# Moving every tile that a rounded float32 matmul reads to a multiple of 512 bytes

## The chip, the cores and the metric

The kernel runs on one core of one Trainium2 chip. The metric is the device time of one launch in microseconds (us). A difference of about 0.2%, some 3.5 us here, is the least that a measurement of this kernel can tell from no change.

## What is computed

The reference is a trunk of two layers on 1,024 tokens of width 1,024, in float32. Each layer is `h = h + W_out(mixer(rmsnorm(h)) * silu(gate))`, and a last norm follows. Layer 0 is a state-space mixer, layer 1 a retention mixer:

```
h = x
for i in range(DEPTH):                      # DEPTH = 2
    hn = _rmsnorm(h, norm_g)
    y = _ssd_mixer(hn, *p) if i == 0 else _retention_mixer(hn, positions, *p)
    h = h + y
return _rmsnorm(h, final_norm)
...
z, xbc, dt = _split(h @ w_in, (SSD_DI, SSD_CONV_DIM, SSD_HEADS))   # layer 0: 1024 -> 6176
q, k, v, g = _split(h @ w_in, (1024, 1024, 2048, 2048))            # layer 1: 1024 -> 6144
return y.astype(h.dtype) @ w_out                                   # both: 2048 -> 1024
```

Layer 0 puts `xbc` through a convolution of four taps and runs 8 groups of heads over 8 chunks of 128 tokens. Layer 1 rotates `q` and `k` and runs 4 heads over the same chunks, carrying a 256 x 512 state per head.

## The kernel before

**Three matmuls for one product.** To come near float32 with matmuls that read a rounded float32 (the type `float32r`), both operands are split: ACT writes the rounded value `hi`, DVE the rest `lo = src - hi` (`split`, L102 to L104). `mm3` (L137 to L140) then adds `hi*hi` (L138), `hi*lo` (L139) and `lo*hi` (L140) in one PSUM bank. Each of these matmuls streams 512 columns of the moving operand (2,048 bytes of each partition) past a stationary operand of 128 x 128 (512 bytes of each partition), and each loads its stationary operand anew. The program has 6,576 of them. Its other matmuls (transposes, the mixer of layer 0, sums over partitions) read plain float32 and are 988 in the program.

**Stages.** `Layer0.run` projects with `project` (outputs `fb`, `ip`, `z`; stationary: the weights `w0h`, `w0l`; moving: the activations `hh`, `hl`) and interleaves the mixer. `OutProj.gen` multiplies by the first output matrix (`o0p`; stationary `o0h`, `o0l`; moving `o0yh`, `o0yl`). `Layer1.head` runs per head: `qk_unit` (`q`, `k`; stationary: weights `w1h`, `w1l`; moving: the activations `h1`), `block` (`g`, `v`; here the activations are stationary and the weights move), `front` and `back` (`pS`, `po`; operands `kh`, `kl`, `sh`, `sl`, `qh`, `ql` against `vh`, `vl`, `Sh`, `Sl`). The second `OutProj` ends it (`o1p`).

**Where the tiles lie.** The order of the work is settled when the program is built; pools are laid out then too. A tile takes a multiple of 32 bytes per partition. Pools without a side fill up from address 0, pools with `side="right"` fill down from 229,344. The lowest 16,384 bytes are a scratch for transfers that GpSimd would issue; the kernel has none. Behind it come 128 bytes of constants and the pool `cpool` (L918: `vec`, `con`, `ones_r`, `cst`). So the addresses of the program of before, as remainders of division by 512, are:

| pool | tiles that `mm3` reads | remainder |
|---|---|---|
| `gp` (from 19,552) | `w0h w0l o0h o0l o1h o1l`, two of five pairs of `w1h w1l` | 96 |
| `actp` (from 52,320) | `hh hl`, most of `o0yh o0yl` | 96 |
| `sbL` (from 52,320) | `vh vl kh kl sh sl qh ql Sh Sl` | 96 |
| `gB` (from 111,008) | three of five pairs of `w1h w1l` | 416 |
| `xs` (from 196,320), eight slots of 4,128 bytes | four of the `h1`, some of `o0yh o0yl o1yh o1yl` | 224, 256, ... 448 |
| `hp` (below `xs`) | the other `h1`, most of `o1yh o1yl` | 224 |
| `tmp0` (below `hp`) | one pair `o0yh o0yl` | 192 |

Within a tile every operand starts at a multiple of 512 bytes. Of the 6,576 matmuls, 3,392 have a moving and a stationary operand with the same remainder, always 96 (`fb` 48, `ip` 1,488, `z` 768, `o0p` 624, `po` 264, `pS` 168, `o1p` 32). In the other 3,184 the two remainders differ (`g` 768, `v` 768, `o1p` 736, `q` 384, `k` 384, `o0p` 144). Below, the first are called in step and the second out of step.

Of the kernel before, what the change touches and what calls it, by code (L numbers as in the profile page):

```python
# [12 lines left out]
F32 = mybir.dt.float32  # L13
# [7 lines left out]
P = 128  # L21
T = 1024
D = 1024
KT = D // P
NC = T // P
# [12 lines left out]
NV = 296  # L38
CO = dict(ident=0, tri=128, rowq=256, rowk=288, inv=320)
NCONST = 321  # L40


def two_pi_parts(bits, count):
# [53 lines left out]
def drain(gen):  # L97
    for _ in gen:
        pass
# [5 lines left out]


class WStream:
    """Weight tiles, loaded and split ahead of their use."""

    def __init__(self, nc, cx, srcs, ahead, name, pools=None):  # L110
        self.nc, self.cx, self.srcs, self.ahead, self.name = nc, cx, srcs, ahead, name
# [31 lines left out]
class Layer0:  # L143
# [28 lines left out]
        return self.sb.tile(shape, F32, tag=tag, bufs=bufs, name=name)  # L172

    def xtile(self, name):
        return self.cx.xs.tile([P, T + 3], F32, tag="xs", bufs=8, name=name)

    def load_x(self):
        nc, cx = self.nc, self.cx
# [5 lines left out]
        self.hl = [cx.act.tile([P, T], F32R, tag="act", bufs=16, name=f"hl{k}") for k in range(KT)]  # L184

    def split_x(self, h):
        """Half of the tokens: load, gain, split."""
        nc, cx = self.nc, self.cx
        sl = slice(h * HALF, (h + 1) * HALF)
        if h == 0:  # L190
            self.wdt = self.tile([P, KT * SSD_H], "xdt", 2, "wdt")
            nc.scalar.dma_start(self.wdt, cx.wdt)
        for k in range(KT):
            nc.sync.dma_start(self.xr[k][:, sl], cx.xT[k][:, sl])
            if h == 0 and k == 3:
                self.ws.prep()
            if h == 0 and k == 7:
                nc.sync.dma_start(cx.con, cx.con_src)
                self.ws.prep()
        if h == 0:  # L200
            for k in range(KT):
                gain = cx.vec[:, VO["n0"] + k : VO["n0"] + k + 1]
                ws = slice(k * SSD_H, (k + 1) * SSD_H)
                nc.vector.tensor_scalar(self.wdt[:, ws], self.wdt[:, ws], gain, None, ALU.mult)
        for k in range(KT):
            xs = self.xr[k][:, sl]
            gain = cx.vec[:, VO["n0"] + k : VO["n0"] + k + 1]
            nc.scalar.activation(self.hh[k][:, sl], xs, AF.Copy, scale=gain)
            nc.vector.scalar_tensor_tensor(
                self.hl[k][:, sl], xs, gain, self.hh[k][:, sl].bitcast(F32), ALU.mult, ALU.subtract  # L210
            )
# [27 lines left out]
        return pt  # L239

    def dt_project(self, h):
        """Sums over every fourth block of channels, in the four quarters of the partitions."""
        nc = self.nc
        sl = slice(h * HALF, (h + 1) * HALF)
        pt = self.dt_ps[h] = self.ps.tile([P, HALF], F32, tag="py", bufs=2, name=f"dt{h}")
        for k in range(KT):
            q = k % 4
            nc.tensor.matmul(
                pt[32 * q : 32 * q + 32], self.wdt[:, k * SSD_H : (k + 1) * SSD_H], self.xr[k][:, sl],
                start=k < 4, stop=k >= 4,  # L250
            )
# [234 lines left out]
    def norm(self, g, lo, hi):  # L486
# [23 lines left out]
        yield  # L510

    def run(self, tail, start):
        """All groups; `tail` is merged with the end of the last one."""
        nc, cx = self.nc, self.cx
        self.load_x()
        self.split_x(0)
        self.dt_project(0)
        self.squares(0)
        first, second = self.units([("B", 0)]), self.units([("C", 0)])
        self.first_banks = [self.ps.tile([P, HALF], F32, tag="pa", bufs=2, name=f"fb{i}") for i in range(2)]  # L520
        next(first)
        next(second)
        self.stats(0)
        self.split_x(1)
        self.dt_project(1)
        self.squares(1)
        next(first)
        next(second)
        self.stats(1)
        drain(first)  # L530
        drain(second)
        merge((self.decay(), 3), (self.units(self.steps[0][2:]), 8))
        for g in range(SSD_G - 1):
            lst = self.steps[g + 1]
            gens = [(self.ssd(g), 9), (self.units(lst), 2 * len(lst))]
            if g:
                gens.append((self.norm(g - 1, 0, T), 4))
            merge(*gens)
        g = SSD_G - 1
        s = self.ssd(g)  # L540
        start()
        merge((take(s, 5), 5), (self.units(self.steps[g + 1]), 4), (self.norm(g - 1, 0, T), 4))
        merge((take(s, 2), 2), (self.norm(g, 0, HALF), 3), (take(tail, 1), 1))
        merge((s, 2), (take(tail, 3), 3))
        merge((self.norm(g, HALF, T), 3), (tail, 4))
        self.es.close()
# [48 lines left out]


class Rope:
    """cos and sin of position times frequency, [frequency, token]."""

    def __init__(self, tc, cx, sb, tmp):  # L600
        self.nc, self.cx, self.tmp = tc.nc, cx, tmp
# [39 lines left out]
class Layer1:  # L641
# [5 lines left out]
        self.h, self.acc = {}, {}  # L647

    def take_h(self, h, d, pt):
        """The first out-projection's results: residual sum, split, squares."""  # L650
        nc, cx = self.nc, self.cx
        sl = slice(h * HALF, (h + 1) * HALF)
        res = cx.tp.tile([P, HALF], F32, tag="res", bufs=2, name=f"res{h}_{d}")
        nc.sync.dma_start(res, cx.xT[d][:, sl])
        nc.vector.tensor_tensor(res, res, pt, ALU.add)
        nc.sync.dma_start(cx.h1d[d][:, sl], res)
        gain = cx.vec[:, VO["n1"] + d : VO["n1"] + d + 1]
        pool, tag, bufs = (cx.xs, "xs", 8) if h == 0 and d < 4 else (self.hpool, "h1", 12)
        ht = pool.tile([P, 2, HALF], F32R, tag=tag, bufs=bufs, name=f"h1_{h}_{d}")
        nc.scalar.activation(ht[:, 0, :], res, AF.Copy, scale=gain)  # L660
        nc.vector.scalar_tensor_tensor(ht[:, 1, :], res, gain, ht[:, 0, :].bitcast(F32), ALU.mult, ALU.subtract)
        self.h[h, d] = ht
        sq = cx.tp.tile([P, HALF], F32, tag="sq", bufs=2, name=f"hsq{h}_{d}")
        nc.scalar.activation(sq, res, AF.Square)
        if d:
            nc.vector.tensor_tensor(sq, sq, self.acc[h], ALU.add)
        self.acc[h] = sq
# [20 lines left out]
    def start(self):  # L688
        tc, cx = self.tc, self.cx
        self.es = ExitStack()  # L690
        self.ps = self.es.enter_context(tc.tile_pool(name="psL", bufs=1, space=PSUM))
        self.sb = self.es.enter_context(tc.tile_pool(name="sbL", bufs=1, reuse_waits="tile"))
        self.gB = self.es.enter_context(tc.tile_pool(name="gB", bufs=1, reuse_waits="tile"))
        seq = []
        for h in range(RH):
            seq += [cx.w1qk[4 * h + i] for i in range(4)]
            seq += [cx.w1g[4 * h + i] for i in range(4)]
            seq += [cx.w1v[4 * h + i] for i in range(4)]
        self.ws = WStream(self.nc, cx, seq, 1, "w1", [(cx.gp, 2), (self.gB, 3)])
# [164 lines left out]


class Final:
    """The second out-projection's results: residual sum and the last norm."""

    def __init__(self, tc, cx, sb, outT):
        self.nc, self.cx, self.sb, self.outT = tc.nc, cx, sb, outT  # L870
# [40 lines left out]
def body(tc, aps):  # L911
    nc = tc.nc
# [4 lines left out]
    with ExitStack() as es:  # L917
        cpool = es.enter_context(tc.tile_pool(name="cpool", bufs=1))  # L918
# [6 lines left out]
        cx.vec = cpool.tile([P, NV], F32, name="vec")  # L925
        cx.con = cpool.tile([P, NCONST], F32, name="con")
        nc.sync.dma_start(cx.vec, aps["vec"])
# [2 lines left out]
        cx.ones = cx.ones_r.bitcast(F32)  # L930
        nc.gpsimd.memset(cx.ones, 1.0)
        cst = cpool.tile([P, 3], F32, name="cst")
        for i, (nm, v) in enumerate((("eps", EPS), ("eps4", 4 * EPS), ("halfpi", math.pi / 2))):
            nc.gpsimd.memset(cst[:, i : i + 1], v)
            setattr(cx, nm, cst[:, i : i + 1])
        cx.ysp = [cx.dram.tile([P, T], F32, name=f"ysp{k}") for k in range(16)]
        cx.osp = [cx.dram.tile([P, T], F32, name=f"osp{k}") for k in range(16)]
        cx.h1d = [cx.dram.tile([P, T], F32, name=f"h1d{k}") for k in range(KT)]
        cx.xs = es.enter_context(tc.tile_pool(name="xs", bufs=1, side="right"))

        act_es = ExitStack()
# [2 lines left out]
        l1 = Layer1(tc, cx)  # L944
# [10 lines left out]
        hpool = es.enter_context(tc.tile_pool(name="hp", bufs=1, side="right", reuse_waits="tile"))  # L955
        with tc.tile_pool(name="tmp0", bufs=1, side="right", reuse_waits="tile") as tmp:
            l1.hpool = hpool
            l1.rnat = hpool.tile([P, NC], F32, name="rnat")
            l1.rope = rope = Rope(tc, cx, hpool, tmp)
            slot = (tmp, "early", 2)  # L960
            op0.early = [(slot, slot)]
            op0.raw = lambda h: (tmp, "yraw", 3)
            merge((take(g0, 7), 7), (rope.half(0), 3))
            drain(take(g0, 5))
            merge((take(g0, 4), 4), (l1.stats(0), 2))
            merge((take(g0, 6), 6), (rope.half(1), 3))
            drain(g0)
# [8 lines left out]
        xs, h1, sg = (cx.xs, "xs", 8), (hpool, "h1", 12), (l1.sb, "Sf", 1)  # L976
# [14 lines left out]
def pack(i):  # L991
# [35 lines left out]
    out["vec"] = v  # L1027
    con = np.zeros((P, NCONST), f)
    con[:, CO["ident"] : CO["ident"] + P] = np.eye(P)
# [11 lines left out]

# [15 lines left out]
```

## Time and profile before

| | us |
|---|---|
| median of 3 runs | 1775.35 |
| lowest and highest | 1774.92 and 1775.7 |
| span of the profiled execution | 1772.9 |

The span runs from the first to the last instruction; the 2.45 us between it and the median lie around it. PE is the matmul engine and PEld its weight loads; DVE, ACT and POOL are the vector, scalar and GpSimd engines, SP issues most transfers. The duration of a matmul in the profile contains the time that it takes to come out of the array; matmuls overlap, so the step from the start of one to the start of the next is what a matmul costs, and it is shorter than the duration. In a steady run the duration is the step plus about 162 ns, so a difference of two durations is a difference of two steps.

### The profile page before, as it was taken

What the parts mean: (1) busy time and instruction counts of PE and PEld (TensorE: products, weight loads), DVE (VectorE), ACT (ScalarE), POOL (GpSimd) and SP (SyncE); (2) the same over time, 40 slices, a digit from 0 to 9 for tenths busy, and PEclk for the clock granted to TensorE, in tenths of its full rate; (3) what the DMA queues carried; (4) which work ended last, traced back from release to release, by engine and by line L of the source; (5) the groups of instructions that cost most, each with busy time, mean ns of one, the idle gap of its engine ahead of it and who ended that gap; (6) DMA issues with size and microseconds to landing.
All of it is one profiled execution on the core that took longest, in us unless ns stands there. A gap on an engine that the chain in (4) does not pass through costs nothing.

```text
span 1772.9 us, 21526 instructions
## 1 busy us (share of the span) xinstructions
PE 1728.8 (98%) x8158; PEld 1381.9 (78%) x8158; DVE 1087.5 (61%) x1889; ACT 687.8 (39%) x1106; POOL 194.4 (11%) x221
## 2 busy tenths in 40 slices
PE   8989999999999999999999999999999999999996
PEld 5777777777878787688878887888888888878785
DVE  7857876868686868878452366246615661666443
ACT  6455544454545455544331232133212322342422
POOL 3012222222222322300000000000000000000000
PEclk9999999999999999999999999999999999999998
DMA  5143322322333334565431112112111221344451
GB/s 179 52 114 85 84 96 72 95 72 96 85 82 96 77 91 115 171 213 184 149 107 36 48 42 66 36 54 65 48 33 45 66 66 48 97 141 143 143 184 71
DMA packets 91766, 166.07 MB, mean 94 GB/s; under 512 B 8592, under 2 KB 42000, under 8 KB 91664
## 3 DMA queue, kind: packets, MB, share of 16 engines
q1 hardware_dynamic: 90368, 162.49, 29.9%
q10 hardware_dynamic: 1296, 2.23, 0.3%
q8 instruction: 64, 1.05, 0.2%
q14 instruction: 38, 0.31, 0.1%
HBM read 139.38 MB, written 25.30 MB: 93 GB/s over the span
## 4 chain that ended last, share of the span: by engine, by line
PE 67%; DVE 11%; DMA 10%; ACT 8%; issue 3%; SPq 1%; DVEq 0%; ACTq 0%
DMA eab<-acd 4%; PE o1p L140 3%; PE o1p L138 3%; PE g L140 3%; PE g L138 3%; PE g L139 3%; PE o1p L139 3%; PE v L139 3%; PE v L138 3%; PE v L140 3%; DMA acb<-acd 3%; PE ip L139 3%; PE ip L140 3%; PE ip L138 3%; DVE acc L341 3%
## 5 line engine op out<-in xcount | busy, mean ns | idle before, releaser
L138 PE MATMUL ip<-hh,w0h 128*128 128x512 f32 x496 | 201.4, 406 | 0.0
L140 PE MATMUL ip<-hh,w0l 128*128 128x512 f32 x496 | 196.6, 396 | 0.0
L139 PE MATMUL ip<-hl,w0h 128*128 128x512 f32 x496 | 195.0, 393 | 0.0
L104 DVE TENSOR_TENSOR w1l<-w1r,w1h 128x1024 fp32r<-128x1024 f32 x48 | 58.3, 1222 | 149.9 <-ACT w1h L103 149.6
L341 DVE SCALAR_TENSOR_TENSOR acc<-pre,vec,acc 128x1024 f32<-128x1024 f32 x96 | 124.5, 1299 | 7.2 <-ACT acc L339 6.6
L459 POOL TENSOR_TENSOR yT<-yT,tof 128x128 f32<-128x128 f32 x112 | 108.2, 987 | 162.6 <-DVE tof L455 162.6
L422 ACT ACTIVATE acb<-acb,acum 128x128 f32<-128x128 f32 x256 | 77.0, 388 | 99.5 <-DMA acb<-acd 99.5
L905 POOL TENSOR_TENSOR h<-h,frs 128x512 f32<-128x512 f32 x2 | 2.9, 1486 | 1018.1 <-ACT frs L899 1018.1
L140 PEld LDWEIGHTS ip<-hh,w0l 128*128 128x128 f32 x496 | 93.2, 188 | 19.9 <-issue 0.7
L138 PEld LDWEIGHTS ip<-hh,w0h 128*128 128x128 f32 x496 | 93.3, 188 | 19.4 <-issue 1.1
L139 PEld LDWEIGHTS ip<-hl,w0h 128*128 128x128 f32 x496 | 93.3, 188 | 18.5 <-DVE xr L223 0.2
L138 PE MATMUL z<-hh,w0h 128*128 128x512 f32 x256 | 103.2, 403 | 1.4 <-DVE w L357 1.4
L103 ACT CAST w1h<-w1r 128x1024 fp32r<-128x1024 f32 x48 | 49.9, 1049 | 136.6 <-PE q L139 51.6
L138 PE MATMUL v<-w1h,h 128*128 128x512 f32 x256 | 102.5, 401 | 0.0
L138 PE MATMUL o0p<-o0yh,o0h 128*128 128x512 f32 x256 | 101.0, 395 | 1.3 <-ACT o0yh L103 1.0
L139 PE MATMUL o0p<-o0yl,o0h 128*128 128x512 f32 x256 | 100.5, 393 | 1.5 <-DVE o0yl L104 1.5
L140 PE MATMUL o1p<-o1yh,o1l 128*128 128x512 f32 x256 | 101.5, 397 | 0.3 <-DVE o1l L104 0.3
L140 PE MATMUL o0p<-o0yh,o0l 128*128 128x512 f32 x256 | 101.2, 395 | 0.3 <-DVE o0l L104 0.3
L139 PE MATMUL v<-w1l,h 128*128 128x512 f32 x256 | 101.5, 397 | 0.0
L138 PE MATMUL g<-w1h,h 128*128 128x512 f32 x256 | 101.2, 395 | 0.0
L138 PE MATMUL o1p<-o1yh,o1h 128*128 128x512 f32 x256 | 101.0, 395 | 0.2 <-DVE vl L764 0.2
L140 PE MATMUL v<-w1h,h 128*128 128x512 f32 x256 | 101.1, 395 | 0.0
(244 smaller groups left out, 4075.0 us busy)
## 6 DMA issues: line engine op xcount, KB each, us to landing
w0r<-w SPq DMA_DIRECT2D x48, 512.0 KB, 3.3
acb<-acd SPq DMA_DIRECT2D x16, 1024.0 KB, 8.6
o0r<-w0o SPq DMA_DIRECT2D x32, 512.0 KB, 3.5
o1r<-w1o SPq DMA_DIRECT2D x32, 512.0 KB, 3.3
eab<-acd SPq DMA_DIRECT2D x64, 128.0 KB, 9.0
o0yr<-ysp SPq DMA_DIRECT2D x32, 256.0 KB, 3.5
w1r<-w1qk SPq DMA_DIRECT2D x16, 512.0 KB, 3.3
w1r<-w1g SPq DMA_DIRECT2D x16, 512.0 KB, 3.4
```

Of the source, the lines that this page charges most:

```text
L103: nc.scalar.copy(hi, src)
L104: nc.vector.tensor_tensor(lo, src, hi.bitcast(F32), ALU.subtract)
L138: nc.tensor.matmul(ps, ahi, bhi, start=first, stop=False)
L139: nc.tensor.matmul(ps, ahi, blo, start=False, stop=False)
L140: nc.tensor.matmul(ps, alo, bhi, start=False, stop=last)
L341: nc.vector.scalar_tensor_tensor(acc, pre[:, j : j + T], cw(j), acc, ALU.mult, ALU.add)
L422: nc.scalar.activation(m[:, h, :], m[:, h, :], AF.Relu, scale=-1.0, bias=self.acum[:, col + h : col + h + 1])
L459: nc.gpsimd.tensor_tensor(yT[j][:, cs], yT[j][:, cs], tof[:, j], ALU.add)
L905: nc.gpsimd.tensor_tensor(r, r, rs, ALU.mult)
```

## The change

No instruction is added on purpose. The scratch shrinks from 16,384 to 1,024 bytes. Three padding tiles are allocated and never used: `pad` (1,952 bytes) at the end of `cpool`, `rpad` (2,016 bytes) at the top of the right side, `spad` (192 bytes) between `sbL` and `gB`. The slots of `xs` grow from 1,027 floats (4,128 bytes) to 1,152 floats (4,608 bytes, 9 x 512); `rnat` grows from 8 floats to 128 (512 bytes). By the same layout, `cpool` now ends at 6,144 (12 x 512), `xs` starts at 190,464 (372 x 512), and each pool of the table above starts at a multiple of 512: all 6,576 matmuls have the remainder 0 in both operands.

```diff
+SCRATCH = 1024
+XS = 1152
+PAD = 1952
+RPAD = 2016
...
     def xtile(self, name):
-        return self.cx.xs.tile([P, T + 3], F32, tag="xs", bufs=8, name=name)
+        return self.cx.xs.tile([P, XS], F32, tag="xs", bufs=8, name=name)
...
         self.sb = self.es.enter_context(tc.tile_pool(name="sbL", bufs=1, reuse_waits="tile"))
+        self.es.enter_context(tc.tile_pool(name="spad", bufs=1)).tile([P, 48], F32, name="spad")
         self.gB = self.es.enter_context(tc.tile_pool(name="gB", bufs=1, reuse_waits="tile"))
...
         cst = cpool.tile([P, 3], F32, name="cst")
+        cpool.tile([P, PAD // 4], F32, name="pad")
...
+        rpad = es.enter_context(tc.tile_pool(name="rpad", bufs=1, side="right"))
+        rpad.tile([P, RPAD // 4], F32, name="rpad")
         cx.xs = es.enter_context(tc.tile_pool(name="xs", bufs=1, side="right"))
...
-            l1.rnat = hpool.tile([P, NC], F32, name="rnat")
+            l1.rnat = hpool.tile([P, P], F32, name="rnat")
...
-    nc = bacc.Bacc("TRN2", target_bir_lowering=False, num_devices=1)
+    nc = bacc.Bacc("TRN2", target_bir_lowering=False, num_devices=1, dynamic_dma_scratch_size=SCRATCH)
```

## Rows read from the trace of the kernel before

**Rows 1.** The page: busy time of the engines, the granted clock, the chain.

```profile
PE 1728.8 (98%) x8158; PEld 1381.9 (78%) x8158; DVE 1087.5 (61%) x1889; ACT 687.8 (39%) x1106; POOL 194.4 (11%) x221
...
PEclk9999999999999999999999999999999999999998
...
PE 67%; DVE 11%; DMA 10%; ACT 8%; issue 3%; SPq 1%; DVEq 0%; ACTq 0%
```

**Rows 2.** PE's waits (total us, times, longest): the costliest of 17 lines.

```profile
PE pst L462 <- ACT bn L417: 13.2, 9, 3.0
```

**Rows 3.** Busy us (instructions) of each engine: layer 0, layer 1's heads.

```profile
50.00:740.00 690.00, 670.46 (x3469) 534.73 (x3468) 512.92 (x839) 338.42 (x603) 173.64 (x192) 1.00 0.33 91
...
880.00:1590.00 710.00, 707.20 (x3202) 574.24 (x3200) 351.75 (x751) 194.32 (x310) 0.00 (x0) 1.00 0.20 63
```

**Rows 4.** PE in order of time (start, duration, us): a run in step.

```profile
67.64 0.39 PE L138 MATMUL ip<-hh,w0h 128*128 128x512 f32 x1
...
73.08 0.39 PE L138 MATMUL ip<-hh,w0h 128*128 128x512 f32 x1
```

**Rows 5.** The same view: a run of `g`, out of step.

```profile
1138.95 0.39 PE L138 MATMUL g<-w1h,h 128*128 128x512 f32 x1
...
1150.13 0.39 PE L138 MATMUL g<-w1h,h 128*128 128x512 f32 x1
```

**Rows 6.** Busy us of each engine in these two runs, columns as above.

```profile
1138.95:1150.13 11.18, 11.18 (x49) 9.03 (x48) 0.00 (x0) 1.38 (x2) 0.00 (x0) 1.00 0.01 1
67.64:73.08 5.44, 5.44 (x25) 4.50 (x24) 5.08 (x7) 2.56 (x5) 0.00 (x0) 1.00 0.31 96
```

**Rows 7.** PE in order of time: a run of `k`, out of step.

```profile
1088.82 0.39 PE L138 MATMUL k<-h,w1h 128*128 128x512 f32 x1
...
1094.14 0.40 PE L140 MATMUL k<-h,w1l 128*128 128x512 f32 x1
```

**Rows 8.** Groups by line, xcount | busy us, mean ns | idle: in step.

```profile
L140 PE MATMUL z<-hh,w0l 128*128 128x512 f32 x256 | 100.1, 391 | 0.0
L139 PE MATMUL z<-hl,w0h 128*128 128x512 f32 x256 | 100.1, 391 | 0.0
...
L139 PE MATMUL pS<-vl,kh 128*128 128x512 f32 x56 | 21.9, 391 | 0.0
...
L139 PE MATMUL po<-Sl,qh 128*128 128x512 f32 x56 | 21.8, 390 | 0.0
```

**Rows 9.** The same view: groups out of step.

```profile
L140 PE MATMUL o1p<-o1yh,o1l 128*128 128x512 f32 x256 | 101.5, 397 | 0.3 <-DVE o1l L104 0.3
L139 PE MATMUL v<-w1l,h 128*128 128x512 f32 x256 | 101.5, 397 | 0.0
...
L140 PE MATMUL v<-w1h,h 128*128 128x512 f32 x256 | 101.1, 395 | 0.0
L140 PE MATMUL g<-w1h,h 128*128 128x512 f32 x256 | 101.0, 395 | 0.0
...
L139 PE MATMUL g<-w1l,h 128*128 128x512 f32 x256 | 100.9, 394 | 0.0
L139 PE MATMUL o1p<-o1yl,o1h 128*128 128x512 f32 x256 | 100.9, 395 | 0.0
...
L140 PE MATMUL q<-h,w1l 128*128 128x512 f32 x128 | 50.5, 394 | 0.0
...
L139 PE MATMUL k<-h,w1h 128*128 128x512 f32 x128 | 50.4, 393 | 0.0
```

**Rows 10.** Plain float32, 512 columns: four records merged, and each one's duration.

```profile
299.89 1.88 PE L501 MATMUL pn<-nsq,ones_r 128*128 128x512 f32 x4
...
L501 PE MATMUL pn<-nsq,ones_r x32: 591/592/594, 213.0 to 745.6; 128*128 128x512 f32 x32
```

**Rows 11.** DMA queues: packets, MB, share of 16 engines.

```profile
q1 hardware_dynamic: 90368, 162.49, 29.9%
q10 hardware_dynamic: 1296, 2.23, 0.3%
```

More of the change, by code (lines that the diff above doesn't have):

```diff
@@ L40 @@
 NCONST = 321
+SCRATCH = 1024
+LINE = 2048
+XS = 1152
+PAD = 1952
+RPAD = 2016
 def two_pi_parts(bits, count):
```

## The prediction

> **What bounds the kernel now.** I read the page first: PE is busy 98% of the span, its clock is granted in full in every slice but the last, and PE has 67% of the chain that ended last [rows 1]. Then PE's waits: the costliest takes 13.2 us in nine times [rows 2], and 44 us of the span in all are left idle by 1728.8 us of busy time. Then the stages side by side. In layer 0 (50 to 740 us) PE is busy 670.46 of 690 us with DVE at 512.92; in the heads of layer 1 (880 to 1590 us) 707.20 of 710 us, with DVE at 351.75 and ACT at 194.32 [rows 3]. So PE's own pace sets the time, in layer 1 with nothing else near. The change removes no instruction and touches no wait; it can act only through how long an operation takes when its operands lie elsewhere. The question is therefore what a step of PE costs in step and out of step.
>
> **The step, in step.** From the first start to the last, 24 steps of `ip` take 73.08 - 67.64 = 5.44 us, 226.7 ns each [rows 4]. Both operands lie 96 bytes past a multiple of 512. At 2.4 GHz this is 544 cycles for 512 columns.
>
> **The step, out of step.** 48 steps of `g` take 1150.13 - 1138.95 = 11.18 us, 232.9 ns each [rows 5]: 6.2 ns more. 23 steps of `k` take 1094.14 - 1088.82 = 5.32 us, 231.3 ns: 4.6 ns more [rows 7]. Two other causes can be set aside. It is not company: during the 48 steps of `g` DVE did nothing and ACT 1.38 of 11.18 us, while during those of `ip` DVE was busy 5.08 of 5.44 us; the clock was 1.00 in both [rows 6]. And it is not the stage: `pS` and `po` run in the same heads as `g` and `v`, but lie at 96 and 96, and show 391 and 390 ns like `z` of layer 0 (391) [rows 8], where `g`, `v`, `q`, `k` and `o1p` show 393 to 397 [rows 9]. Nor is it the role of an operand: in `q` and `k` the weights are stationary, as in `z`, and they take longer like `g`, where the weights move. What separates the two kinds of groups is that the two remainders are equal or not. I read this as two streams out of one memory, the moving columns of one matmul and the weights that PEld fetches for the next, which hinder each other least when they start at the same place of a 512-byte stretch. The trace shows the price; the reason is my guess.
>
> **The change part by part.**
>
> *In step already, 3,392 matmuls.* They go from 96 and 96 to 0 and 0. The remainders stay equal, so I take 226.7 ns to stay: 0 us. The bounds: no row has an operand at 0. Upwards the price is that of the slow groups, 4.5 ns x 3,392 = 15 us; downwards the nearest row is the plain float32 matmul, whose four records start 0.43 us apart ((1.88 - 0.592) / 3) [rows 10], that is 1,030 cycles for 512 columns taken at two cycles each, 215 ns for 512 cycles. A step can't be expected below that, so the gain here is at most 3,392 x 11.7 = 40 us. I take nothing, because the row nearest to it is the one in step.
>
> *Out of step, 3,184 matmuls.* They become in step. From the means of the groups against 391 [rows 8, 9]: `g` (394.5) 3.5 ns x 768 = 2.7 us; `v` (396) 5 x 768 = 3.8; `o1p` (396) 5 x 736 = 3.7; `q` (394) 3 x 384 = 1.2; `k` (393) 2 x 384 = 0.8; `o0p`'s 144, which have no row of their own, at 4.5 ns, 0.6: 12.8 us. This is the low end, because 391 holds the disturbed steps behind a bank's emptying too. The high end is the clean run of `g` against that of `ip`: 6.2 x 3,184 = 19.7 us [rows 4, 5]. I take 4.5 ns, which the run of `k` gives and which lies between the ends' 4.0 and 6.2: 4.5 x 3,184 = 14.3 us.
>
> *On the path or beside it.* Nearly all of the 14.3 us falls in the heads and in the second output projection, where PE idles 2.8 of 710 us and DVE and ACT have half of the time or more to spare [rows 3]; a PE that is 2% faster there wakes no new bound. I count it in full.
>
> *The padding tiles, the smaller scratch, the wider slots.* No instruction, no transfer. The scratch would serve transfers issued by GpSimd; 90,368 and 1,296 packets went over the two hardware queues that carry the kernel's transfers [rows 11]. Cost 0; if a transfer used the scratch after all, it would be one that the profile doesn't show. DVE, ACT and POOL read tiles at new places too; if they slowed by 1%, layer 0 would feel it first, where DVE has 177 us of 690 to spare [rows 3], so the cover is wide and I count 0.
>
> *The plain float32 matmuls, 988.* They need 0.43 us for 512 columns, within 1% of two cycles a column [rows 10], although their operands lie at 224 and 64: no price of place to give back. 0.
>
> Sum: -14.3 us on the profiled execution (1772.9 to 1758.6); the 2.45 us around the span stay, so 1775.35 - 14.3 = 1761.0 us.
>
> **The rule that speaks against it.** The rows say that a step depends on where the weights of the next matmul lie. The Trainium skill, TensorE: Matmul & The Clock Gate, Part 2 (step ①), says the opposite: the moving operand and the weight load have read ports of their own, and loading the next weights takes no bandwidth from the running matmul. By that rule the sum of this change would be 0. [...]
>
> **The rivals.**
>
> *Nothing changes: 1775.* (The rule above would give this time.) The difference between the groups is that of something that goes with the remainders, such as which pool an operand is in. For it: all the groups out of step have an operand in `xs`, `hp`, `gB` or `tmp0`, those in step none. Against it: one cause would have to act in the same way in tiles of four pools in both roles. Also here: the order of the instructions or the layout isn't what I worked out, and the gain is spent.
>
> *A multiple of 512 is worth more than equality.* 544 cycles are 32 more than the columns. If these come from the start inside a stretch (2,048 bytes from 96 on touch five stretches of 512, from 0 four), all 6,576 steps fall. In full, to the 215 ns of the plain passes: 11.7 x 6,576 = 77 us beyond the 14.3, of which layer 0's share (2,304 x 11.7 = 27 us) may be eaten by DVE in part; 1685 to 1700. In part, by a quarter of the 32 cycles (one boundary of four), 3.3 x 6,576 = 22 us: 1739. For it: no row contradicts it, since no operand lies at 0. Against it: shorter steps would help at 256 or 128 too, and `h1` in `xs` at 256 and 352 is moved in the run of `k` without a step below 226.7 on average [rows 7].
>
> *Slower: 0 and 0 collide.* What makes 96 and 96 good is not equality but the start inside a stretch: with both at 0 the two streams open the same stretch at the same instant and meet at each boundary. Then the steps in step rise by the price of being out of step, 4.5 x 3,392 = 15.3 us, and the others stay: 1790. It decides as soon as a step of `ip` in a steady run is above 232 ns. For it: nothing but the missing row. Against it: two starts at 96 meet each boundary together as well.
>
> **How the numbers follow.** The forecast gets 0.62, with its own range 1755 to 1763 from the two ends of the sum. More than equality: 0.18, half of it near 1739, half near 1690. No change 0.12, slower 0.08. Faster by over 0.2% (3.5 us, about the least that a measurement of this kernel can tell) is the first two: 0.80; within it 0.12; slower 0.08. The range leaves out the full case (0.09) and the slower one (0.08): it goes from 1738, which takes in the partial case, to 1778, which takes in no change.
>
> **What the profile would show.** If I am right: `g`, `v`, `q`, `k` and `o1p` at 389 to 392 ns, a run of `g` at 226.7 ns a step, `z` and `ip` as before, PE's share of the span unchanged and the heads 10 us shorter. `z` below 388 means that 512 itself counts; `z` above 394 that 0 and 0 collide; `g` at 394 that the remainder was never the cause. I am wrong in the size if the steps equal 226.7 but waits grow by what they give back, which I would see in layer 0 first.

## The result, and the profile after

| | before | after |
|---|---|---|
| median of 4 runs, us | 1775.53 | 1759.68 |
| lowest and highest | 1774.92 and 1777.26 | 1758.45 and 1760.73 |
| profiled execution, us | 1775.35 | 1760.33 |
| its span, us | 1772.9 | 1758.5 |

The ratio is 0.990, with a 95% interval of 0.9888 to 0.9913: about 15.9 us faster. The forecast was 1761.0 us, and 1758.6 for the span. On each engine the instructions stand in the same order as before.

The page of the changed kernel, its first lines (`mm3` is at L144 to L146 now):

```profile
PE 1717.0 (98%) x8158; PEld 1383.0 (79%) x8158; DVE 1088.2 (62%) x1889; ACT 687.6 (39%) x1106; POOL 192.2 (11%) x221
```

PE has the same number of matmuls and is busy 11.8 us less; its share is 98% as before [rows 1]. DVE and ACT read and write all their tiles at new places and take the same time to within 1 us.

The groups of matmuls by line (count | busy us, mean ns | idle):

```profile
L145 PE MATMUL v<-w1l,h 128*128 128x512 f32 x256 | 100.3, 393 | 0.0
L146 PE MATMUL z<-hh,w0l 128*128 128x512 f32 x256 | 100.1, 391 | 0.0
...
L146 PE MATMUL v<-w1h,h 128*128 128x512 f32 x256 | 100.1, 391 | 0.0
L146 PE MATMUL o1p<-o1yh,o1l 128*128 128x512 f32 x256 | 100.1, 392 | 0.4 <-DVE o1l L110 0.4
L146 PE MATMUL g<-w1h,h 128*128 128x512 f32 x256 | 99.7, 389 | 0.0
L145 PE MATMUL g<-w1l,h 128*128 128x512 f32 x256 | 99.6, 389 | 0.0
...
L145 PE MATMUL o1p<-o1yl,o1h 128*128 128x512 f32 x256 | 99.5, 389 | 0.0
...
L146 PE MATMUL q<-h,w1l 128*128 128x512 f32 x128 | 49.9, 390 | 0.0
...
L145 PE MATMUL k<-h,w1h 128*128 128x512 f32 x128 | 49.8, 389 | 0.0
```

The groups that showed 393 to 397 [rows 9] show 389 to 393; `z` was at 391 [rows 8] and stays there. The same in PE's order of time, for the run of `k` of rows 7 and for 48 steps of `g` as in rows 5 (start, duration):

```profile
1085.69 0.39 PE L144 MATMUL k<-h,w1h 128*128 128x512 f32 x1
...
1090.91 0.39 PE L146 MATMUL k<-h,w1l 128*128 128x512 f32 x1
...
1139.96 0.39 PE L146 MATMUL g<-w1h,h 128*128 128x512 f32 x1
...
1150.84 0.39 PE L146 MATMUL g<-w1h,h 128*128 128x512 f32 x1
```

The 48 steps of `g` take 10.88 us, 226.7 ns each, where they took 232.9; the 23 steps of `k` take 5.22 us, 227.0 ns, where they took 231.3. Where the time went is read from the first and the last start of a stage's matmuls (count: shortest, median, longest ns, first to last start). Before:

```profile
L138 PE MATMUL o0p<-o0yh,o0h x256: 387/389/794, 706.6 to 900.4; 128*128 128x512 f32 x128
...
L138 PE MATMUL q<-h,w1h x128: 388/393/798, 901.1 to 1424.1; 128*128 128x512 f32 x128
...
L138 PE MATMUL o1p<-o1yh,o1h x256: 387/393/502, 1561.9 to 1756.0; 128*128 128x512 f32 x128
...
L140 PE MATMUL o1p<-o1yh,o1l x256: 387/395/793, 1564.2 to 1756.4; 128*128 128x512 f32 x128
```

After:

```profile
L144 PE MATMUL o0p<-o0yh,o0h x256: 387/389/792, 706.4 to 899.8; 128*128 128x512 f32 x128
...
L144 PE MATMUL q<-h,w1h x128: 389/389/791, 900.4 to 1416.7; 128*128 128x512 f32 x128
...
L144 PE MATMUL o1p<-o1yh,o1h x256: 387/389/504, 1552.1 to 1741.8; 128*128 128x512 f32 x128
...
L146 PE MATMUL o1p<-o1yh,o1l x256: 387/389/792, 1554.5 to 1742.2; 128*128 128x512 f32 x128
```

| stretch, from first start to first start | before | after | difference | out of step before x 4.5 ns |
|---|---|---|---|---|
| start and layer 0 (to `o0p`) | 706.6 | 706.4 | -0.2 | 0 |
| first output projection (to `q`) | 194.5 | 194.0 | -0.5 | -0.6 (144) |
| heads of layer 1 (to `o1p`) | 660.8 | 651.7 | -9.1 | -10.4 (2,304) |
| second output projection (to its last start) | 194.5 | 190.1 | -4.4 | -3.3 (736) |
| sum | | | -14.2 | -14.3 (3,184) |

The gain lies where the matmuls were out of step. The heads' 9.1 us are those of this one execution, in which PE idled 4.2 us of them after 2.3 before; when the changed kernel was run again (below), they took 650.1 us, 10.7 less than before. Layer 0 needs a closer look, since its clock wasn't the same. Two stretches of 3.4 us of the trace after, and between them what came ahead of the second (columns as in rows 3):

```profile
105.70:109.10 3.40, 3.40 (x17) 2.55 (x16) 1.01 (x2) 1.44 (x5) 0.00 (x0) 0.50 0.54 181
254.00:259.20 5.20, 3.33 (x16) 2.41 (x14) 1.22 (x3) 3.99 (x7) 0.00 (x0) 1.00 0.18 68
259.30:262.70 3.40, 3.40 (x15) 2.36 (x14) 3.40 (x7) 1.47 (x3) 0.00 (x0) 0.50 0.15 22
```

PE had been idle 1.9 of the 5.2 us before the second one, and then ran 3.4 us at half of its clock (1.2 GHz). The profiled execution of before has the clock in full at these places. Twice 3.4 us at half are about 3.4 us of work lost, and yet layer 0 took as long as before: its costliest wait fell by 2.4 us, from 13.2 [rows 2] to

```profile
PE pst L468 <- ACT bn L423: 10.8, 9, 2.5
```

So layer 0 has some give in its waits. The comparisons of medians below are over several executions and don't hang on where such a stretch falls in one.

### The profile page after: what moved, and what is told of

The parts are those of the page before. It is cut to its first block, busy times and chain, and to the rows that moved or that the text cites. A ratio compares the mean times of both kernels' runs of the same rounds, so it can differ in the third digit from the quotient of the medians.

```text
span 1758.5 us, 21524 instructions
## 1 busy us (share of the span) xinstructions
PE 1717.0 (98%) x8158; PEld 1383.0 (79%) x8158; DVE 1088.2 (62%) x1889; ACT 687.6 (39%) x1106; POOL 192.2 (11%) x221
## 4 chain that ended last, share of the span: by engine, by line
PE 53%; DVE 3%; DMA 3%; ACT 2%; issue 1%; SPq 0%; DVEq 0%; ACTq 0%
PE o1p L146 3%; PE g L146 3%; PE g L144 3%; PE o1p L144 3%; PE g L145 3%; PE o1p L145 3%; PE v L144 3%; PE v L145 3%; PE v L146 3%; PE o0p L145 3%; PE o0p L146 3%; PE o0p L144 3%; PE k L145 2%; PE k L146 2%; PE k L144 2%; PE q L144 1%
## 5 line engine op out<-in xcount | busy, mean ns | idle before, releaser
L144 PE MATMUL ip<-hh,w0h 128*128 128x512 f32 x496 | 202.3, 408 | 0.0
L146 PE MATMUL ip<-hh,w0l 128*128 128x512 f32 x496 | 197.4, 398 | 0.0
L146 PEld LDWEIGHTS ip<-hh,w0l 128*128 128x128 f32 x496 | 93.7, 189 | 20.3 <-issue 0.7
L144 PEld LDWEIGHTS ip<-hh,w0h 128*128 128x128 f32 x496 | 93.7, 189 | 19.5 <-issue 1.1
L144 PE MATMUL z<-hh,w0h 128*128 128x512 f32 x256 | 103.4, 404 | 1.4 <-DVE w L363 1.4
L144 PE MATMUL o0p<-o0yh,o0h 128*128 128x512 f32 x256 | 100.8, 394 | 1.3 <-ACT o0yh L109 1.0
L146 PE MATMUL o0p<-o0yh,o0l 128*128 128x512 f32 x256 | 101.1, 395 | 0.5 <-DVE o0l L110 0.4
L144 PE MATMUL v<-w1h,h 128*128 128x512 f32 x256 | 101.5, 397 | 0.0
L146 PE MATMUL o1p<-o1yh,o1l 128*128 128x512 f32 x256 | 100.1, 392 | 0.4 <-DVE o1l L110 0.4
L146 PE MATMUL z<-hh,w0l 128*128 128x512 f32 x256 | 100.1, 391 | 0.0
L145 PE MATMUL z<-hl,w0h 128*128 128x512 f32 x256 | 100.1, 391 | 0.0
L146 PE MATMUL v<-w1h,h 128*128 128x512 f32 x256 | 100.1, 391 | 0.0
```

What stands on the lines that cost most here:

```text
L144: nc.tensor.matmul(ps, ahi, bhi, start=first, stop=False)
L145: nc.tensor.matmul(ps, ahi, blo, start=False, stop=False)
L146: nc.tensor.matmul(ps, alo, bhi, start=False, stop=last)
```

## The experiments

The theory: the cost is in the unequal start of the two operands, and equality is all that counts. The rivals: the multiple of 512 counts by itself; or the cause is something else that goes with the pools. What was open besides: whether "equal" means equal within 512 bytes, and whether the price of a step comes out on the clock in every stage. All but the two benches are the changed kernel with one or two numbers or lines altered, or none; no operation is added or taken away.

**Equal, but at no multiple of 512.**

```diff
-PAD = 1952
-RPAD = 2016
+PAD = 2112
+RPAD = 1856
```

> All tiles that a rounded float32 matmul reads lie at remainder 160 by 512 instead of 0; both operands of all 6,576 matmuls stay equal. Equality theory (what counts is that the moving operand and the next stationary operand have the same remainder): as after the change, 1760 us, runs of g and ip at 226.7 ns a step. A multiple of 512 counts by itself: the gain of the change is lost in part or whole, 1765 to 1790 us, and steps of g above 229 ns.

Measured: 1765.08 us (1763.66 to 1770.06) beside 1781.22 for the kernel before on the same chip; ratio 0.9919 (0.9899 to 0.9938). The groups by line:

```profile
L146 PE MATMUL z<-hh,w0l 128*128 128x512 f32 x256 | 100.1, 391 | 0.0
...
L145 PE MATMUL g<-w1l,h 128*128 128x512 f32 x256 | 99.6, 389 | 0.0
```

`g` stands at 389 and `z` at 391, as with all operands at 0. The gain is that of equality; the multiple of 512 adds nothing.

**Unequal by 256.**

```diff
-RPAD = 2016
+RPAD = 1760
```

> The pools on the right side (xs, hp, tmp0) lie at remainder 256, all others at 0: the same 3,184 matmuls as before the change have unequal remainders, by 256. Equality by 512: 3,184 x 3 to 4.5 ns come back, 1769 to 1774 us, with the means of g, v, k and o1p at 393 to 396 ns. Equality by 256 would do: 1760 us, means at 389 to 391 ns.

Measured: 1762.34 us (1760.87 to 1762.99), ratio 0.9898 (0.9878 to 0.9917). The groups by line:

```profile
L145 PE MATMUL g<-w1l,h 128*128 128x512 f32 x256 | 99.6, 389 | 0.0
...
L146 PE MATMUL k<-h,w1l 128*128 128x512 f32 x128 | 49.8, 389 | 0.0
```

The tiles of the right side lie 256 bytes away from the others modulo 512, and nothing is lost. The stretch within which starts must be equal is 256 bytes long (or a part of that), not 512; the bench below, in which 64 and 128 apart cost something, leaves 256.

**Unequal by 32.**

```diff
-RPAD = 2016
+RPAD = 1984
```

> The pools on the right side lie at remainder 32, all others at 0: 3,184 matmuls are out of step by 32 bytes, the least that the layout allows. Equality theory: 3,184 x 4.5 ns come back, 1772 to 1776 us. Nearness would do (two starts within 64 bytes are as good as equal): 1760 us.

Measured: 1782.42 us (1779.29 to 1789.34), ratio 1.0013 (1.0000 to 1.0026). The groups by line:

```profile
L146 PE MATMUL g<-w1h,h 128*128 128x512 f32 x256 | 101.2, 395 | 0.0
...
L146 PE MATMUL z<-hh,w0l 128*128 128x512 f32 x256 | 100.2, 391 | 0.0
...
L146 PE MATMUL k<-h,w1l 128*128 128x512 f32 x128 | 50.6, 395 | 0.0
```

One number moved by 32 takes the whole gain away, in the 3,184 matmuls whose operands lie on two sides and in no others. Against the mean of the two runs above (1763.7, on the same chip) it costs 18.7 us, or 5.9 ns for each of them: more than the 14 expected. In this layout every one of these steps is unequal by the same 32 bytes, and that is a dear distance, as the bench below shows. The smaller scratch, the pads and the wider slots are all in this kernel too, so they are not the cause of the gain.

**Without the pad between `sbL` and `gB`.**

```diff
-        self.es.enter_context(tc.tile_pool(name="spad", bufs=1)).tile([P, 48], F32, name="spad")
```

> The changed kernel without the padding tile between sbL and gB: gB lies at remainder 320, and 1,344 matmuls of the heads (864 with the weights moving, 480 with them stationary) are out of step by 320, all others in step. Equality theory: 1,344 x 4.5 = 6 us come back, 1764 to 1767 us, all of it in g, v, q and k, while o1p stays at 389 to 392 ns. If the gain came from something else than the remainders, such as the pools on the right side alone: 1760 us.

Measured: 1769.36 us (1766.48 to 1774.35), ratio 0.9942 (0.9923 to 0.9961): 5.7 us above the 1763.7, where 6 were expected. The groups by line:

```profile
L146 PE MATMUL g<-w1h,h 128*128 128x512 f32 x256 | 100.5, 393 | 0.0
...
L146 PE MATMUL k<-h,w1l 128*128 128x512 f32 x128 | 50.4, 394 | 0.0
```

The cost goes by the count: 1,344 matmuls out of step instead of 3,184, 4.2 ns each on the medians. `o1p`, which is in step here, stays at 389 to 392.

**The step by itself.** A kernel that does blocks of 72 matmuls into one bank and nothing beside them (both layers are left out, so its own time says nothing):

```diff
+        for b, (nm, mo, wo, m, n) in enumerate(BLOCKS):
+            pt = ps.tile([P, 512], F32, tag="mm", bufs=4, name=nm)
+            for i in range(REPS):
+                if nm in ("ha", "hb"):
+                    mo, wo = 96 * (i % 2), 96 * (i % 2 if nm == "ha" else 1 - i % 2)
+                w0 = wo // 4 + 128 * (i % 8)
+                nc.tensor.matmul(
+                    pt[:m, :n], wt[:, w0 : w0 + m], mov[:, mo // 4 : mo // 4 + n], start=i == 0, stop=i == REPS - 1
+                )
```

> The layers are left out: 25 blocks of 72 rounded float32 matmuls each run one after the other with nothing beside them, to price a step by the place of its operands alone. Blocks da to dn: stationary at 0, moving at 0, 16, 32, 64, 96, 128, 160, 192, 224, 256, 320, 384, 448, 480. Equality theory: da at 226.7 ns a step, all others 229 to 235. Blocks ea (96 and 96), eb (256 and 256): 226.7; if a multiple of 512 counts by itself they are longer than da. ec and ed (moving 0, stationary 96 and 256): 229 to 235. Whose stationary operand counts: in ha each matmul has the remainder of its own and not of the next, in hb that of the next and not its own. If the fetch for the next matmul is what collides, hb is at 226.7 and ha above 229; if its own counts, the reverse. Where the 32 cycles beyond the 512 columns come from: fa and fb have stationary operands of 64 and 32 columns. If each column of weights fetched costs a quarter of a cycle, 16 and 8 cycles remain (220 and 217 ns); if the 32 cycles are fixed, 226.7. ga streams 256 columns: 120 ns if the 32 cycles are fixed.

The last matmuls of some blocks in PE's order of time, drawn together (first start, time to the last end, count):

```profile
30.97 11.04 PE L954 MATMUL da<-mov,wt 128*128 128x512 f32 x48
...
64.12 11.36 PE L954 MATMUL dc<-mov,wt 128*128 128x512 f32 x48
...
80.82 11.38 PE L954 MATMUL dd<-mov,wt 128*128 128x512 f32 x49
...
181.34 11.04 PE L954 MATMUL dj<-mov,wt 128*128 128x512 f32 x48
...
264.54 11.04 PE L954 MATMUL ea<-mov,wt 128*128 128x512 f32 x48
...
297.40 11.41 PE L954 MATMUL ec<-mov,wt 128*128 128x512 f32 x48
...
377.89 6.16 PE L954 MATMUL ga<-mov,wt 128*128 128x256 f32 x50
...
389.27 11.63 PE L954 MATMUL ha<-mov,wt 128*128 128x512 f32 x49
...
406.02 11.44 PE L954 MATMUL hb<-mov,wt 128*128 128x512 f32 x49
```

Less one duration (0.39 us) and divided by the steps, `da` gives (11.04 - 0.39) / 47 = 226.6 ns, `dc` 233.3, `dd` 228.9. In this way, for all blocks (128 stationary columns unless told):

| block | moving, stationary (bytes) | step, ns |
|---|---|---|
| `da`, `ea`, `eb` | 0, 0; 96, 96; 256, 256 | 226.7 |
| `dj`, `ed` | 256, 0; 0, 256 | 226.7 |
| `dd`, `dk` | 64, 0; 320, 0 | 228.9 |
| `db` | 16, 0 | 231.7 |
| `dl` | 384, 0 | 232.2 |
| `dc`, `de` to `di`, `dm`, `dn` | 32, 96 to 224, 448, 480; 0 | 233.3 to 234.3 |
| `ec` | 0, 96 | 234.3 |
| `fa`, `fb` | 0, 0 with 64 and 32 stationary columns | 230.0 and 231.7 |
| `fc` | 96, 0 with 32 stationary columns | 233.4 |
| `ga` | 0, 0 with 256 moving columns | 120.0 |
| `ha` | each matmul's own starts equal, the next weights' not | 234.0 |
| `hb` | the next weights' start equal, its own not | 230.0 |

The price is there with no other engine at work and no other pool: company and pool are excluded as causes. It vanishes at equal starts (at 0, 96 and 256, the places tried), and also at 256 apart; 64 apart costs a third of the full 6.6 ns. In `ha` each matmul is equal within itself and yet pays in full, so equality with its own weights is not enough; `hb`, where each matmul's starts equal those of the next weights, pays half (230.0), while by the prediction's guess it would pay nothing. `fa` and `fb`, expected at 220 and 217 ns or at 226.7, are at neither.

**Out of step in layer 0.** In the heads PE is the bound by far. To see whether the price is paid where DVE works beside, the activations of layer 0 are moved by 128 (and with them the tiles of `sbL`, which take their place later and lie alike among themselves):

```diff
+        es.enter_context(tc.tile_pool(name="apad", bufs=1)).tile([P, 32], F32, name="apad")
...
-        self.es.enter_context(tc.tile_pool(name="spad", bufs=1)).tile([P, 48], F32, name="spad")
+        self.es.enter_context(tc.tile_pool(name="spad", bufs=1)).tile([P, 16], F32, name="spad")
```

> The changed kernel with 128 bytes of padding ahead of actp (and 128 fewer behind sbL): now layer 0 and the first output projection are out of step, by 128 (2,960 matmuls: ip, z and fb 2,304, o0p 624, o1p 32), and g, v, q, k and nearly all of o1p stay in step. If what counts is whether the two remainders differ, 2,960 x 6.2 = 18 us come on top of the changed kernel, in layer 0 (14 us) and o0p (4 us): 1777 to 1780 us on the chip where the changed kernel takes 1760, with z and ip at 396 or more. If DVE's work in layer 0 covers a longer step, the steps grow and the stage doesn't: 1764 to 1768 us. If the gain of the change had to do with layer 1's pools only: 1760 us.

The changed kernel itself once more, on the same chip beside it:

> The changed kernel once more, beside the kernels of this call on one chip: a ratio to the kernel before of 0.989 to 0.992, and steps of 226.7 ns in g and ip.

Measured: 1769.08 us (1766.88 to 1771.45), ratio 0.994 (0.9926 to 0.9953), and 1761.82 us (1758.99 to 1763.15), ratio 0.9899 (0.9885 to 0.9912), with 1779.63 for the kernel before: the move costs 7.3 us, within the 4 to 8 expected if DVE's work covers a longer step, and far from the 18 expected in full. With the activations moved, by line:

```profile
L145 PE MATMUL z<-hl,w0h 128*128 128x512 f32 x256 | 101.3, 396 | 0.0
```

By stage, first with the activations moved and then the changed kernel itself:

```profile
L144 PE MATMUL o0p<-o0yh,o0h x256: 387/392/798, 715.2 to 910.6; 128*128 128x512 f32 x128
```

```profile
L144 PE MATMUL o0p<-o0yh,o0h x256: 387/389/792, 707.1 to 899.9; 128*128 128x512 f32 x128
...
L144 PE MATMUL q<-h,w1h x128: 389/389/791, 900.6 to 1415.3; 128*128 128x512 f32 x128
...
L144 PE MATMUL o1p<-o1yh,o1h x256: 387/389/501, 1550.7 to 1740.4; 128*128 128x512 f32 x128
...
L146 PE MATMUL o1p<-o1yh,o1l x256: 388/389/792, 1553.1 to 1740.9; 128*128 128x512 f32 x128
```

PE's wait for `bn`, in the same order:

```profile
PE pst L468 <- ACT bn L423: 8.0, 8, 2.2
```

```profile
PE pst L468 <- ACT bn L423: 10.9, 7, 2.6
```

The stretches of layer 0 at half of the clock, in the same order (columns as in rows 3):

```profile
112.60:119.40 6.80, 5.46 (x21) 4.36 (x22) 4.57 (x12) 6.80 (x16) 0.61 (x1) 0.50 0.00 1
262.90:266.30 3.40, 3.40 (x15) 2.20 (x14) 3.40 (x6) 1.91 (x3) 0.00 (x0) 0.52 0.00 0
```

```profile
113.60:117.00 3.40, 3.40 (x12) 2.63 (x11) 1.48 (x3) 3.40 (x9) 0.15 (x1) 0.51 0.00 0
```

`z` goes from 391 to 396. Over the clean starts of the two traces (steps from one start to the next below 250 ns) the steps of layer 0 rise from 228.5 to 232.4 ns and those of the first output projection, of which 624 in 768 are out of step, from 227.2 to 232.2: 2,304 x 3.9 = 9.0 us and 768 x 5.0 = 3.8 us, 12.8 us of longer steps. On the medians 7.3 us of them come out, somewhat over half; the two intervals leave some 3 us either way, so that all of them come out is excluded. By stage, from one profiled execution of each: the first output projection takes 195.4 instead of 192.8 us from first to last start, 2.6 of the 3.8 us that lie there. Layer 0 has 9.0 us of them and ends 8.1 us later. In that execution PE was busy 8.9 us at half of the clock, in the other 3.4; half of the difference, some 3 us, is the clock's. About 5 of the 9.0 us remain, and the waits for `bn` gave 2.9 us back. One pair of executions does not show this split: in the traces of the four other layouts above, where no matmul of layer 0 is out of step, layer 0 took 710.1 to 713.8 us. The half on the medians stands without it. That DVE's work is what hides the rest is not shown.

**Which matmuls are concerned.** A second bench of the same kind (both layers left out), with other types and other orders of starts:

```diff
+                if nm == "hc":
+                    wo = 96 * (i % 2)
+                if nm == "hd":
+                    mo = 96 * (i % 2)
+                if nm == "he":
+                    mo, wo = 96 * (i // 4 % 2), 96 * (i // 4 % 2)
...
+                ww, mm = (raw, raw2) if nm[0] == "j" else (wth, movh) if nm[0] == "k" else (wt, mov)
```

> The layers are left out again: blocks of 72 matmuls with nothing beside them. hc: moving always at 0, stationary at 0 and 96 in turn; the step is long (231 to 234) where the next matmul's stationary is at 96, if the fetch for the next is what collides, and where its own is at 96 otherwise. hd: moving at 0 and 96 in turn, stationary at 0. he: both at 0 for four matmuls, then both at 96 for four; 226.7 but for one step in four. ia and ib: the same stationary columns at every matmul, moving at 0 and at 96; 226.7 and 233 if a fetch is made each time all the same. ja and jb: plain float32, moving at 0 and at 96: 430 ns both, as the prediction took its place to be free. ka and kb: bfloat16: if the 32 cycles are the price of 4-byte columns at one a cycle, 213 to 216 ns in both; if they belong to each load of weights, 226.7.

Blocks of plain float32 in PE's order of time, drawn together as above:

```profile
145.89 41.79 PE L965 MATMUL ja<-raw,raw 128*128 128x512 f32 x97
...
207.69 41.79 PE L965 MATMUL jb<-raw,raw 128*128 128x512 f32 x97
```

Blocks of bfloat16 by tile (count: shortest, median, longest ns, first to last start; of 72 matmuls one or two have no record):

```profile
L965 PE MATMUL ka<-movh,wth x70: 379/379/379, 249.3 to 264.6; 128*128 128x512 bf16 x70
...
L965 PE MATMUL kb<-movh,wth x71: 379/379/380, 264.9 to 280.2; 128*128 128x512 bf16 x71
```

Plain float32 takes (41.79 - 0.59) / 96 = 429 ns for each pass over 512 columns, with the moving operand at 0 (`ja`) and at 96 (`jb`). Bfloat16 takes 15.3 / 71 = 215 to 216 ns at 0 (`ka`) and at 96 (`kb`). Of the three types only the rounded float32 asks for equal starts, at the one distance tried. Its price stays when the stationary operand is the same in every matmul: 226.7 ns (`ia`) and 233.3 (`ib`); the trace has a load of weights for each of them all the same. The blocks with changing starts settle nothing on whose weights count: `hc` (moving 0, stationary 0 and 96 in turn) and `hd` (the other way round) both take 230.0 ns, and `he`, equal in every matmul but changing place after every four, 232.5, where three steps in four were expected at 226.7. A change of place from one matmul to the next may cost by itself; that is not shown.

## Why the prediction was right

**The bound.** Right: in layer 1 PE is the bound, and what its steps lost came off the end: from the first start of `o0p` to the last of `o1p` the changed kernel took 14.0 us less than before, and 16.0 less when run again (193.5, 650.1 and 190.2 us by stage), where the steps lost 15.9 (below).

**The step.** Right in its reading: the difference between the groups was that of the starts, not of company, stage or role. The bench shows 226.7 and 233.3 ns with nothing beside PE. In size it was a little low. Over the clean starts of `q`, `k`, `g`, `v` and `o1p` the step took 232.3 ns before and 227.3 after: 5.0 ns, not 4.5, and 3,184 x 5.0 = 15.9 us, what the medians show. The run of `k`, which the 4.5 was said to come from, gives 4.6. The 5.0 is an average over the distances of the old layout. A layout with one dear distance pays 5.9 (unequal by 32), one with distances of 64 and 192 pays 4.2 on the medians (without the pad; 5.4 by the clean starts of its trace). The high end of the range, 6.2, lies between the 5.9 and the bench's 6.6 for a dear distance, and need be no error of the trace.

**In step already: 0 us.** Right for the bulk: `z` at 391 before, after and with all at 160; over clean starts `ip` goes from 228.3 to 228.6 ns and `z` from 227.9 to 228.3, under 1 us in all. An exception is small: `pS`, with both operands at 96 before, fell from 229.5 to 227.3 ns (168 matmuls, 0.4 us). It runs between matmuls of `v`, which lay elsewhere before and lie alike now; with the activations moved by 128, where it lies apart from them again, it shows 230.0. So the places of the neighbours seem to count too.

**Counted in full.** Right for the heads and the output projections. It would have been wrong for layer 0, where no matmul was out of step; there a longer step comes out by about half, as far as the medians tell, although PE is busy 97% of it too [rows 3]. PE's share alone doesn't tell how much of a longer step comes out.

**Pads, scratch, plain float32: 0 each.** Right: DVE 1088.2 us after 1087.5, and the plain float32 matmul shows 429 ns at both places.

**The stretch of 512 bytes.** Wrong as a detail: starts 256 apart are as good as equal ones. The prediction took the 512 from the change and from the one remainder that it saw; the rows that it went by do not tell 512 from 256. The sum didn't hang on it.

**The reason.** The guess was that the columns of a matmul and the fetch of the next weights hinder each other. That it isn't the matmul's own weights is spoken for by `ha` (own equal, 234.0 ns); that it is the next ones is not shown, since `hb` (230.0) should then be at 226.7, `hc` and `hd` fit both, and `he` (232.5) fits neither. The rows did not say, as the prediction has it, that the weights of the next matmul are those that count; they show that unequal places cost. The reason stays open.

**The rule that spoke against it.** With nothing else at work and the moving operand at 0, the step is 226.7 or 234.3 ns by the place of the weights alone (`da` and `ec`). The Trainium skill, TensorE: Matmul & The Clock Gate, Part 2 (step ①), by which loading the next weights takes no read bandwidth from the running matmul, leaves no room for such a difference; for rounded float32 the measurement decides against it, though which fetch is in the way stays open. The formula that the same page of the Trainium skill gives for one matmul by itself (Back-to-back issue gap: N / 2.4 + 2.5, 215.8 ns for 512 columns) agrees with the bfloat16 of the second bench, 215 to 216 ns, and with no step of rounded float32; the about 131 ns that the section gives for a stream of weight loads and matmuls shows in no run here.

**The rivals.** That nothing changes falls with the result and with the run unequal by 32. That a multiple of 512 counts by itself falls with all at 160 and with `ea` and `eb` of the bench. That 0 and 0 collide falls with `z` at 391 and `da` at 226.7. On the sum, -14.3 us was forecast for the span and -14.4 came, which is in part luck: the 4.5 was low by a tenth, and the execution that was profiled after the change idled more in the heads than the one before. The medians are 15.9 us apart, 1.5 more than the spans; 0.6 of that is the time around the span (1.8 us after, 2.45 before), and the rest is the spread of single executions.

## What to carry to other kernels

Where rounded float32 matmuls follow each other closely, let the moving and the stationary operands all start at the same place modulo 256 bytes; a few unused tiles between pools do it, and it was worth 0.9% here. To see whether a kernel has the trouble, subtract two starts in a steady run of matmuls: the step should be the columns plus 32 cycles (226.7 ns for 512), and a mean duration that differs from one pool to another, at the same clock, is a sign. Multiply a price per step in full only where nothing waits beside PE; in a stage with some give, move one operand on purpose and measure what comes out.

## What the runs showed of the hardware

- Rounded float32 costs 32 cycles beyond its columns at best, for 512 columns (226.7 ns, 544 cycles of 2.4 GHz) as for 256 (120.0 ns, 288 cycles); bfloat16 took 215 to 216 ns for 512, at most 518 cycles.
- Fewer stationary columns made its step longer, not shorter: 230.0 ns with 64 and 231.7 with 32, at equal starts, though its load of weights took 134 and 107 ns instead of 188.
- The price of place has steps of its own: 0 at a distance of 256 bytes, 2.2 ns at 64 and 320, 5 at 16, 5.5 at 384 and 6.6 or more at the other multiples of 32 tried.
- In the layers PE ran at half of its clock for stretches of 3.4 us or twice that, each time after waits (it was idle for 1.9 of the 5.2 us ahead of the second one shown above); the trace before has none of them, that of the changed kernel two, that of its second run one, and those of the other kernels two to four, all but one in layer 0.
